# An encoder layer on one core: filling matmuls between early products, a group of w_ada loaded before the second claim, early sums and transposes moved forward, and the ramp's second half begun with the late pairs

## The chip, the cores and the metric

The kernel runs on one core of a Trainium2 chip. The metric is device time in microseconds (us). TensorE (PE in the profile) multiplies into PSUM banks, VectorE (DVE) and ScalarE (ACT) read and write SBUF and PSUM, GpSimd (POOL) and SyncE (SP) mostly issue DMAs here. Every engine works through its own queue in order; an instruction at the head of a queue that waits for a semaphore holds up all that stand behind it.

## The reference

One layer of an encoder over x (1024 tokens, 2048 channels), float32 throughout:

```python
mod = silu(c) @ w_ada + b_ada
shift, scale, gate = split(mod, 3)
h = rmsnorm(x, pre_g) * (1 + scale) + shift
q, k, v, gate_a, u, gate_p = split(h @ w_in)
y_a = windowed_gqa(q, k, v, rel_table, sink) * silu(gate_a)
y_p = multiscale_pool(u, w_pool_grp, pool_scale) * silu(gate_p)
g_a, g_p = split(sigmoid(h @ w_merge + b_merge))
o = (g_a * (y_a @ w_br_attn) + g_p * (y_p @ w_br_pool)) @ w_out
return x + gate * rmsnorm(o, post_g)
```

What the change touches is the beginning: mod, h, and the first eighth or so of `h @ w_in`.

## The kernel before, in words

**Numbers.** A float32 operand is split into a high part (rounded, by ACT) and a low part (the rest, by DVE); `split` (L95 to L97) does it. A product takes three matmuls for each 128 rows of k: high by high, high by low, low by high. All large products are Strassen products of two by two blocks (`strassen`, L223): seven block products, with sums of blocks of the weights (on DVE, as they come in) and sums of blocks of the moving operand (`B11`, `T3`, `T2`, `B21`, `T4`, `T1`, `B22`, prepared once). A pair is 256 columns of weights, and its work runs over seven steps (`run`, L336); the last block product of a pair is put off to step 2 of the next (`flush`, L331).

**The rows of k.** The 16 k tiles of h are used as pairs of tiles j = 0 to 7. The first pass over all weights uses j = 0 to 3, the second j = 4 to 7. For h of pair j the kernel needs the columns j of shift and scale, hence a product of silu(c) with group j of w_ada (`modulation`, L484, in four quarters and a column step) and, for all rows, the norms of x (`norm_rows` L414, `scale_rows` L429) and its transposes on PE (`turn_part` L436, `take_turned` L444).

**The start.** To have PE at work before all of x is loaded, the first eight pairs of weights, the ramp, are cut up:
- Pairs 0 to 3 (`AHEAD_PAIRS`) are multiplied with j = 0 alone, in plain block products of six matmuls, `plain_block` (L680), marked PB in the profile. The first token half comes first (`fill_half(0)` makes its operands, loop at L705), then the second (`fill_half(1)`, L714 to L736). Their weights come as two wide tiles (`fetch_wide`, L624; splits in `wide_weights`, L672). ACT or DVE copies each finished bank and POOL's queue stores it to `ramp_d`.
- Pairs 4 to 7 are then multiplied with j = 0 and 1 as Strassen products (loop at L747): the ramp's first half. Meanwhile groups 2 and 3 of w_ada are multiplied in (`late_sums`, L651), and `fill(2)`, `fill(3)` make the operands of j = 2 and 3.
- The ramp's second half (loop at L756) adds the rest: j = 1, 2, 3 for pairs 0 to 3 (nine matmuls a block product) and j = 2, 3 for pairs 4 to 7 (six). It reads the first half's results back from `ramp_d` (`load_parts`, L216).

After that come the other pairs of the first pass, the second pass, attention, pooling, the branches and the output product, none of them touched.

**Queues and buffers.** SP issues nearly all loads and stores, in the program's order where `keep` holds it. Two pools matter. `big` has 56 slots of 128 x 512 floats: transposed rows (12), rows of x (16 for each token half), groups 0, 1, 2 of w_ada (16 each), the operands of j (14, allotted by `claim`, L558, with a memset on POOL), the last six tiles of group 3; a slot that is asked for is that of an earlier tile, and what fills it waits for that tile's last reader. Tiles `raw` (weights as loaded) have four buffers; a pair with two k pairs takes one of them, one with three or four takes two (`load_raws`, L191). The wide tiles are two of the four.

In the order of the program SP has: x first half, wide 0, group 0, wide 1, x second half, group 1, weights of pairs 4 and 5, group 2 (behind `claim(1)`), weights of pair 6, group 3, weights of pair 7; then the stores of the first half; then the weights of all eight pairs of the second half (`ramp_raws`, L750).

Of the kernel before, what the change touches and what calls it, by code (L numbers as in the profile page):

```python
# [16 lines left out]
ALU = mybir.AluOpType  # L17
# [4 lines left out]
P = 128  # L22
# [21 lines left out]
def encoder_layer(ctx: ExitStack, tc: tile.TileContext, x, c, table, w_ada, b_ada, pre_g,  # L44
# [36 lines left out]
    def bank(tag, name="b"):  # L81
        return psum.tile([P, 512], F32, tag=tag, name=uid(name), bufs=1 if tag in SEEDED else 2)
# [8 lines left out]
    def keep(ins):  # L91

        tc.keep_in_program_order(ins)
# [334 lines left out]

    def scale_rows(si, ssq):  # L429
        keep(nc.vector.reciprocal(rstd[:, si:si + 1], ssq[:, 5:6]))  # L430
        keep(nc.vector.tensor_scalar(xts[si, 0], xts[si, 0], rstd[:, si:si + 1], None, op0=ALU.mult))
        keep(nc.scalar.activation(xts[si, 1], xts[si, 1], AF.Copy, scale=rstd[:, si:si + 1]))

    tbanks = {}

# [39 lines left out]
    def ada_slots(j, kcs=range(KT)):  # L475
        tiles = []
        for kc in kcs:
            tiles.append(slot("ada", F32, (P, 4, P)))
            load(tiles[-1].rearrange("p (g h) n -> p g (h n)", g=2),
                 w_ada[kc * P:(kc + 1) * P, 0:2 * D].rearrange("p (g n) -> p g n", g=2)  # L480
                 [:, :, j * 256:(j + 1) * 256])
        return tiles
# [136 lines left out]
    def ramp_raws(i, js):  # L619
        raws.append(load_raws(*weight_of(RAMP_ORDER[i]), rows_in_turn(0), js, True))  # L620
# [3 lines left out]
    def fetch_wide(half):  # L624

        if not wide:
            wide.extend(wp.tile([P, 4, 256], F32, tag="raw", name=uid("wide"), bufs=4) for _ in range(2))
        for kh in range(2):
            n0 = COL_K + half * 512
            keep(load(wide[kh][:, 2 * half:2 * half + 2],  # L630
                      w_in[kh * P:(kh + 1) * P, n0:n0 + 512].rearrange("p (i n) -> p i n", n=256)))

    fetch_rows_of_x(0)
    fetch_wide(0)
    ada = [ada_slots(0)]
    fetch_wide(1)
    claim(0)
    fetch_rows_of_x(1)
    ada.append(ada_slots(1))
    ramp_raws(4, (0, 1))  # L640
    ramp_raws(5, (0, 1))
    claim(1)
    ada.append(ada_slots(2))
# [28 lines left out]
    def wide_weights(i):  # L672
        hi, lo = (wp.tile([P, 2, 256], F32R, tag=t, name=uid(t), bufs=4) for t in ("whi", "wlo"))
        for kh in range(2):
            split(hi[:, kh], lo[:, kh], wide[kh][:, i], True)
        weights0[i] = hi, lo

    blocks = [0]

    def plain_block(i, nt, s, by_vector=False):  # L680

        ps = bank(("mm", "sc")[blocks[0] % 2], "PB")
        whi, wlo = (w[:, :, nt * P:(nt + 1) * P] for w in weights0[i])
        mov = (op["B11"][0], op["B21"][0]) if s == 0 else (right["B12"], op["B22"][0])
        for n, (kh, w, m) in enumerate(((0, whi, 0), (0, wlo, 0), (1, whi, 0), (1, wlo, 0), (0, whi, 1), (1, whi, 1))):
            keep(nc.tensor.matmul(ps, w[:, kh], mov[kh][m], start=n == 0, stop=n == 5, skip_group_check=True))  # L686
        blocks[0] += 1

        def put_by():
            t = ev.tile([P, 512], F32, tag="ev", name=uid("c"))  # L690
            if by_vector:
                keep(nc.vector.tensor_copy(t, ps))
            else:
                keep(nc.scalar.activation(t, ps, AF.Copy))
            nc.gpsimd.dma_start(block(ramp_d[i], 0)(f"{nt + 1}{s + 1}"), t)

        return put_by

    wide_weights(0)
    wide_weights(1)  # L700
    g0 = modulation(0, ada[0].__getitem__, True)
    for step in g0[:4]:
# [12 lines left out]
    early.close()  # L715

# [3 lines left out]
        for k in ks:  # L720
            take_turned(1, k, False)

    plain_block(0, 0, 1)()
    turn_next((2, 3))
    plain_block(0, 1, 1)()
    fill_sums(0)
    plain_block(1, 0, 1)()
    plain_block(1, 1, 1)()
    turn_next((4, 5))
    s0, s1, s2, s3, _ = modulation(1, ada[1].__getitem__, True)  # L730
    plain_block(2, 0, 1)()
    s0()
    plain_block(2, 1, 1)()
    s1()
    plain_block(3, 0, 1)()
    s2()  # L736
    last = plain_block(3, 1, 1)
    s3(last)
    turn_next((6, 7))
    for tag in SEEDED:  # L740
        hi = op["B11"][0][0]
        keep(nc.tensor.matmul(bank(tag, "OPEN"), hi[:, 0:P], hi, start=True, stop=True))
# [12 lines left out]
    pev = ramp.enter_context(pool("rampev", 6))  # L755
    for i in range(RAMP):  # L756
        run(ramp_gen((1, 2, 3) if i in A else (2, 3), i, parts[i], True), side, range(7),
            ((3, lambda i=i: parts.update({i + 1: load_parts(pev, block(ramp_d[i + 1], 0))})),)
            if i < RAMP - 1 else ())
    flush()  # L760
    ramp.close()
    ev_ctx.close()
# [224 lines left out]
    with pool("attn") as ap:  # L987
# [116 lines left out]
        def step(u, e):  # L1104
            nu = len(UNITS)
            if e == 0 and 0 <= u - LAG_V < nu:
                values(u - LAG_V)
            if e == 1 and u % 16 in (1, 3) and u < nu:
                turn_v(u % 16 // 2)
            if e == 1 and 0 <= u - LAG_T < nu:  # L1110
                turn(u - LAG_T, 0)
                turn(u - LAG_T, 1)
            if u < nu:
                if u % 16 == 0 and e == 0:
                    take_k(UNITS[u][0] * 2 // GQA)
                if u % 4 == 0:
                    split_q(e)
                scores(u, e)
            if e == 1:
                if opened:  # L1120
                    gated(*opened.pop())
                if u % 4 == 3 and u + 1 < nu:
                    fetch_q(u + 1)
                c_ = u - LAG_V + 1
                if (c_ + 1) % 16 == 0 and c_ + 1 < nu:
                    fetch_v(UNITS[c_ + 1][0] * 2 // GQA)
                if 0 <= c_ < nu:
                    if c_ % 4 == 0:
                        fetch_gate(c_)
# [530 lines left out]
```

## Time and profile before

| what | us |
|---|---|
| median of 3 runs | 2127.03 (2126.09 to 2128.45) |
| the profiled execution | 2126.26 |
| its span, first to last instruction | 2124.5 |
| DMA traffic | 474.49 MB, mean 223 GB/s |
| DMA queue of SP (q1) | 64.6% of 16 engines |

The page's first part gives each engine's busy time as a share of the span; the windows give the same for any stretch, with the granted clock of TensorE beside it; the timeline gives each group of instructions with the idle time of the engine before it and what ended that. Times in these views count from the span's start. A matmul's shown duration overlaps the next one's, so the cost of one in a row of them is the distance of their starts.

### The profile page before, as it was taken

How to read it: one execution, taken by the hardware profiler on the slowest of the kernel's cores; microseconds unless marked ns; L12 is line 12 of the kernel's file. 1: busy time of each engine (PE TensorE's matmuls, PEld its weight loads, DVE VectorE, ACT ScalarE, POOL GpSimd, SP SyncE). 2: the span in 40 equal slices, each digit the busy share in tenths (PEclk: the TensorE clock that was granted, in tenths of full speed). 3: DMA queues.
4: the chain of work that ended last, by engine and by line, in shares of the span. 5: the costliest groups of instructions: out<-in, count | busy, mean ns of one | idle time of the engine just before them, and what ended most of it. 6: DMA issues, size and time to landing. Idle time of an engine off the chain costs nothing.

```text
span 2124.5 us, 28858 instructions
## 1 busy us (share of the span) xinstructions
PE 2079.3 (98%) x9453; PEld 1706.7 (80%) x9453; DVE 1551.5 (73%) x2783; ACT 1114.9 (52%) x2118; POOL 41.7 (2%) x135
## 2 busy tenths in 40 slices
PE   6989999999999999999999999999999999999998
PEld 3568878788888888888888888888888788888886
DVE  5576768788556776677777678957957977879667
ACT  5553434444474544566666543333645645767554
POOL 1100000000000000000000000010000000000000
PEclk9899999999999999999999999999999999999999
DMA  9846877999686455545544477675754555685996
GB/s 335 302 167 213 277 252 257 316 331 299 203 262 207 133 171 203 166 165 173 176 169 156 139 232 234 220 246 178 236 169 158 186 199 192 213 320 203 296 336 242
DMA packets 304171, 474.49 MB, mean 223 GB/s; under 512 B 24323, under 2 KB 144235, under 8 KB 304020
## 3 DMA queue, kind: packets, MB, share of 16 engines
q1 hardware_dynamic: 297664, 455.70, 64.6%
q0 software_dynamic: 4896, 14.73, 1.8%
q10 hardware_dynamic: 1460, 2.22, 0.3%
q8 instruction: 74, 1.21, 0.2%
q14 instruction: 77, 0.63, 0.1%
HBM read 344.60 MB, written 130.05 MB: 223 GB/s over the span
## 4 chain that ended last, share of the span: by engine, by line
PE 92%; DVE 3%; DMA 3%; ACT 1%; issue 1%; SPq 0%; DVEq 0%; ACTq 0%
PE Z L248 30%; PE V L248 20%; PE X L248 20%; PE Z L1367 2%; PE Z L1369 2%; PE Z L1368 2%; PE V L1369 1%; PE X L1368 1%; PE X L1369 1%; PE V L1368 1%; PE V L1367 1%; PE X L1367 1%; PE GEMV L494 1%; PE PT L1077 1%; PE PB L686 1%; DMA xt<-in_x_dram 1%
## 5 line engine op out<-in xcount | busy, mean ns | idle before, releaser
L96 ACT ACTIVATE whi<-raw 128x512 fp32r<-128x512 f32 (+2 forms) x528 | 319.0, 605 | 532.0 <-PE Z L248 260.8
L97 DVE TENSOR_TENSOR wlo<-raw,whi 128x512 fp32r<-128x512 f32 (+2 forms) x528 | 344.2, 655 | 171.8 <-PE Z L248 130.2
L97 DVE TENSOR_TENSOR wlo<-wr,whi 128x512 fp32r<-128x512 f32 x224 | 150.8, 688 | 51.9 <-ACT whi L96 48.7
L96 ACT ACTIVATE whi<-wr 128x512 fp32r<-128x512 f32 x224 | 138.5, 629 | 87.6 <-DVE wlo L97 32.0
L114 DVE TENSOR_TENSOR raw<-raw,raw 128x512 f32<-128x512 f32 (+1 forms) x80 | 54.7, 683 | 82.5 <-DMA raw<-in_w_merge_dram 60.4
L248 PE MATMUL X<-B11h,whi 128*128 128x512 f32 x332 | 91.6, 394 | 8.9 <-ACT whi L96 8.2
L114 DVE TENSOR_TENSOR u<-V,u 128x512 f32<-128x512 f32 x94 | 64.6, 688 | 40.8 <-PE V L248 40.0
L248 PE MATMUL V<-T3h,whi 128*128 128x512 f32 x332 | 91.3, 394 | 1.9 <-ACT whi L96 1.6
L96 ACT ACTIVATE whi<-ws 128x512 fp32r<-128x512 f32 (+2 forms) x88 | 53.5, 608 | 72.9 <-PE X L248 65.3
L248 PE MATMUL X<-B11l,whi 128*128 128x512 f32 x332 | 91.1, 393 | 0.1
L248 PE MATMUL X<-B11h,wlo 128*128 128x512 f32 x332 | 90.7, 393 | 0.0
L248 PE MATMUL Z<-T2h,wlo 128*128 128x512 f32 x332 | 90.2, 391 | 0.5 <-DVE wlo L97 0.5
L248 PE MATMUL Z<-B22h,whi 128*128 128x512 f32 x332 | 90.6, 392 | 0.0
L248 PE MATMUL Z<-T2h,whi 128*128 128x512 f32 x332 | 90.4, 392 | 0.1
L248 PE MATMUL Z<-T1h,whi 128*128 128x512 f32 x332 | 90.5, 390 | 0.0
L248 PE MATMUL V<-T3l,whi 128*128 128x512 f32 x332 | 90.4, 391 | 0.0
L248 PE MATMUL Z<-T2l,whi 128*128 128x512 f32 x332 | 90.2, 391 | 0.0
L248 PE MATMUL X<-B21h,whi 128*128 128x512 f32 x332 | 90.2, 390 | 0.0
L248 PE MATMUL V<-T3h,wlo 128*128 128x512 f32 x332 | 90.1, 391 | 0.0
L248 PE MATMUL V<-T4l,whi 128*128 128x512 f32 x332 | 90.0, 390 | 0.1
L248 PE MATMUL V<-T4h,whi 128*128 128x512 f32 x332 | 90.1, 391 | 0.0
L248 PE MATMUL Z<-T1l,whi 128*128 128x512 f32 x332 | 89.8, 389 | 0.0
(366 smaller groups left out, 4885.7 us busy)
## 6 DMA issues: line engine op xcount, KB each, us to landing
part<-part_d SPq DMA_DIRECT2D x136, 256.0 KB, 4.6
ada<-in_w_ada_dram SPq DMA_DIRECT2D x128, 256.0 KB, 6.0
raw<-in_w_merge_dram SPq DMA_DIRECT2D x64, 512.0 KB, 5.3
wr<-ws_dS SPq DMA_DIRECT2D x60, 512.0 KB, 5.2
raw<-in_w_in_dram SPq DMA_DIRECT2D x56, 512.0 KB, 4.0
wr<-in_w_out_dram SPq DMA_DIRECT2D x48, 512.0 KB, 4.9
proj_d<-part SPq DMA_DIRECT2D x68, 256.0 KB, 2.3
sw<-in_w_out_dram SPq DMA_DIRECT2D x64, 256.0 KB, 5.1
```

What stands on the lines that cost most here:

```text
L96: ins = (nc.scalar.activation(hi, src, AF.Copy), nc.vector.tensor_tensor(lo, src, f32(hi), ALU.subtract))
L97: nc.vector.tensor_tensor(lo, src, f32(hi), ALU.subtract))
L114: return (eng or nc.vector).tensor_tensor(o, a, b, ALU.add)
L248: nc.tensor.matmul(ps, w_[:, i], op[mov][j][m_], start=fresh and i == 0 and n == 0, stop=i == nj - 1 and n == 2, skip_group_check=True)
L494: ins = nc.tensor.matmul(pv[g:g + 32, :], scz[:, kc, :], tile_of(kc), start=kc < 4, stop=kc >= 12, tile_position=(0, g))
L686: keep(nc.tensor.matmul(ps, w[:, kh], mov[kh][m], start=n == 0, stop=n == 5, skip_group_check=True))
L1077: nc.tensor.transpose(pt[:, i * P:(i + 1) * P], p[:, i * P:(i + 1) * P], ident)
L1367: nc.tensor.matmul(pb, hi, w[0], start=first, stop=False, skip_group_check=True)
L1368: nc.tensor.matmul(pb, lo, w[0], start=False, stop=False, skip_group_check=True)
L1369: nc.tensor.matmul(pb, hi, w[1], start=False, stop=last, skip_group_check=True)
```

## The change

Nothing of what is computed changes. The parts:
- **Filling matmuls.** `warm(n)` multiplies a split weight tile of pair 0 into a bank that nobody reads, n times (128 x 512 each): 3, 3 and 4 between the quarters of group 0's product, 3 behind its column step, 4 and 3 around the last transposes of the second token half. The column step of group 0 now is a step of its own (`apart`).
- **Loads.** `fetch_wide(1)` moves ahead of group 0, and group 2 of w_ada ahead of `claim(1)`.
- **Weight splits.** All four pairs' wide weights are split ahead of group 0's product; before, pairs 2 and 3 were split inside the loop over plain blocks.
- **Row scaling.** Both scaled quarters of a row of x are now scaled by DVE (before, one by DVE and one by ACT); all copies of plain blocks are now made by ACT (before, in the first token half, every second by DVE). The norm of the next rows is now issued behind a pair's plain blocks, the scaling ahead of them.
- **Plain blocks.** `plain_blocks` issues both column halves of a pair together; with `apart` (first pair of each token half) four matmuls of each column half come first and the two with a low part of the operand after.
- **Transposes and sums forward.** In the second token half the order becomes: pair 0, transposes 2 and 3, `fill_sums(0)`, pair 1, transposes 4 and 5, two quarters of group 1, pair 2, transposes 6 and 7, third quarter, the two OPEN matmuls, fourth quarter with pair 3's blocks between its product and its column step.
- **The ramp's second half** runs pairs 4, 5, 6, 7 first and then 0 to 3 (`SECOND`). Its first loads of weights are issued inside the first half, one at step 1 of pairs 5, 6 and 7 and one behind the loop; those of pairs 0 to 3 at step 1 of the third, fifth, sixth and seventh pair of the second half.

```diff
     def scale_rows(si, ssq):
         keep(nc.vector.reciprocal(rstd[:, si:si + 1], ssq[:, 5:6]))
-        keep(nc.vector.tensor_scalar(xts[si, 0], xts[si, 0], rstd[:, si:si + 1], None, op0=ALU.mult))
-        keep(nc.scalar.activation(xts[si, 1], xts[si, 1], AF.Copy, scale=rstd[:, si:si + 1]))
+        for q in range(2):
+            keep(nc.vector.tensor_scalar(xts[si, q], xts[si, q], rstd[:, si:si + 1], None, op0=ALU.mult))
...
     fetch_wide(0)
+    fetch_wide(1)
     ada = [ada_slots(0)]
-    fetch_wide(1)
...
     ramp_raws(5, (0, 1))
+    ada.append(ada_slots(2))
     claim(1)
-    ada.append(ada_slots(2))
...
-    def plain_block(i, nt, s, by_vector=False):
+    def plain_blocks(i, s, apart=False):
...
+        parts_ = ((range(4), range(4, 6)) if apart else (range(6),))
+        for ns in parts_:
+            for nt in range(2):
+                for n in ns:
+                    piece(nt, n)
+                if n == 5:
+                    put_by(nt)
+
+    def warm(n):
+
+        whi = weights0[0][0]
+        for _ in range(n):
+            keep(nc.tensor.matmul(bank("at", "WARM"), whi[:, 0, 0:P], whi.rearrange("p k n -> p (k n)"),
+                                  start=True, stop=True))
+
+    for i in range(AHEAD_PAIRS):
+        wide_weights(i)
+    g0 = modulation(0, ada[0].__getitem__, True, True)
+    for step in g0[:2]:
         step()
+        warm(3)
+    g0[2]()
+    warm(4)
+    g0[3]()
+    g0[4]()
+    warm(3)
     fill_half(0)
+    ssq = norm_rows(4)
     for m in range(4):
-        if m < 2:
-            wide_weights(2 + m)
-        ssq = norm_rows(4 + m)
-        for nt in range(2):
-            plain_block(m, nt, 0, nt == 1)()
         scale_rows(4 + m, ssq)
+        plain_blocks(m, 0, m == 0)
+        if m < 3:
+            ssq = norm_rows(5 + m)
-    for m in range(4):
-        turn_part(1, m, (0, 1), SEEDED)
+    turn_part(1, 0, (0, 1), SEEDED)
+    turn_part(1, 1, (0, 1), SEEDED)
+    turn_part(1, 2, (0, 1), SEEDED)
+    warm(4)
+    turn_part(1, 3, (0, 1), SEEDED)
+    warm(3)
     fill_half(1)
...
+    plain_blocks(0, 1, True)
     turn_next((2, 3))
     fill_sums(0)
+    plain_blocks(1, 1)
     turn_next((4, 5))
     s0, s1, s2, s3, _ = modulation(1, ada[1].__getitem__, True)
     s0()
     s1()
+    plain_blocks(2, 1)
+    turn_next((6, 7))
     s2()
-    last = plain_block(3, 1, 1)
-    s3(last)
-    turn_next((6, 7))
     for tag in SEEDED:
         hi = op["B11"][0][0]
         keep(nc.tensor.matmul(bank(tag, "OPEN"), hi[:, 0:P], hi, start=True, stop=True))
+    s3(lambda: plain_blocks(3, 1))
...
-    for i in range(AHEAD_PAIRS, RAMP):
-        run(ramp_gen((0, 1), i, None, False), side, range(7),
-            ((4, lambda: parts.update({0: load_parts(ev, block(ramp_d[0], 0))})),) if i == RAMP - 1 else ())
-    for i in range(RAMP):
+    SECOND = [*range(AHEAD_PAIRS, RAMP), *A]
+    def second_raws(n):
+        i = SECOND[n]
         ramp_raws(i, (1, 2, 3) if i in A else (2, 3))
+
+    for n, i in enumerate(range(AHEAD_PAIRS, RAMP)):
+        at = [(1, partial(second_raws, n - 1))] if n else []
+        if i == RAMP - 1:
+            at.append((4, lambda: parts.update({SECOND[0]: load_parts(ev, block(ramp_d[SECOND[0]], 0))})))
+        run(ramp_gen((0, 1), i, None, False), side, range(7), at)
+    second_raws(RAMP - AHEAD_PAIRS - 1)
     fill(2)
     fill(3)
...
+    later_raws = {2: 4, 4: 5, 5: 6, 6: 7}
+    for n, i in enumerate(SECOND):
+        at = [(3, lambda i=SECOND[n + 1]: parts.update({i: load_parts(pev, block(ramp_d[i], 0))}))] if n < RAMP - 1 else []
+        if n in later_raws:
+            at.append((1, partial(second_raws, later_raws[n])))
+        run(ramp_gen((1, 2, 3) if i in A else (2, 3), i, parts[i], True), side, range(7), at)
```

More of the change, by code (lines that the diff above doesn't have):

```diff
@@ L678, in encoder_layer, with piece, put_by @@
     blocks = [0]
-    def plain_block(i, nt, s, by_vector=False):
-        ps = bank(("mm", "sc")[blocks[0] % 2], "PB")
-        whi, wlo = (w[:, :, nt * P:(nt + 1) * P] for w in weights0[i])
+    def plain_blocks(i, s, apart=False):
+        whi, wlo = weights0[i]
         mov = (op["B11"][0], op["B21"][0]) if s == 0 else (right["B12"], op["B22"][0])
[L685 to L689, printed above, removed]
+        open_ = []
+        for nt in range(2):
+            open_.append(bank(("mm", "sc")[blocks[0] % 2], "PB"))
+            blocks[0] += 1
+        def piece(nt, n):
+            kh, w, m = ((0, whi, 0), (0, wlo, 0), (1, whi, 0), (1, wlo, 0), (0, whi, 1), (1, whi, 1))[n]
+            keep(nc.tensor.matmul(open_[nt], w[:, kh, nt * P:(nt + 1) * P], mov[kh][m], start=n == 0, stop=n == 5,
+                                  skip_group_check=True))
+        def put_by(nt):
@@ L690, in put_by @@
             t = ev.tile([P, 512], F32, tag="ev", name=uid("c"))
[L691 to L694, printed above, removed]
+            keep(nc.scalar.activation(t, open_[nt], AF.Copy))
             nc.gpsimd.dma_start(block(ramp_d[i], 0)(f"{nt + 1}{s + 1}"), t)
[L697 to L702, printed above, removed]
-        step()
+        parts_ = ((range(4), range(4, 6)) if apart else (range(6),))
@@ new lines, in plain_blocks @@
+        for ns in parts_:
+            for nt in range(2):
+                for n in ns:
[10 more added lines that the diff above has]
+    g0 = modulation(0, ada[0].__getitem__, True, True)
@@ L755, in encoder_layer @@
     pev = ramp.enter_context(pool("rampev", 6))
[L756 to L759, printed above, removed]
+    later_raws = {2: 4, 4: 5, 5: 6, 6: 7}
[4 more added lines that the diff above has]
+        run(ramp_gen((1, 2, 3) if i in A else (2, 3), i, parts[i], True), side, range(7), at)
     flush()
```

7 lines of the change are left out of this document (removed).

## The prediction

> **What bounds the kernel now.** First the page's list of engines.
>
> ```profile
> PE 2079.3 (98%) x9453; PEld 1706.7 (80%) x9453; DVE 1551.5 (73%) x2783; ACT 1114.9 (52%) x2118; POOL 41.7 (2%) x135
> ```
>
> TensorE (PE) is busy for 2079.3 of 2124.5 us. The change removes none of its products, so what can be won is in the 45 us in which it stands, and in stretches where it is busy at a lower clock. Both lie ahead of 144 us. I cut that part into windows (columns: busy time and count of PE, PEld, DVE, ACT, POOL; granted clock; DMA share and GB/s).
>
> ```profile
> 37.70:44.40 6.70, 5.70 (x13) 4.46 (x14) 4.53 (x13) 2.88 (x8) 1.12 (x2) 0.50 1.06 377
> 44.50:54.60 10.10, 8.02 (x39) 6.31 (x37) 8.07 (x25) 8.61 (x23) 3.21 (x6) 1.00 1.08 382
> 54.80:61.50 6.70, 6.12 (x18) 4.55 (x19) 4.81 (x7) 2.23 (x4) 1.01 (x12) 0.50 1.07 380
> 82.10:88.80 6.70, 6.39 (x14) 4.61 (x15) 5.50 (x10) 4.45 (x10) 0.00 (x0) 0.50 1.09 353
> 88.90:130.40 41.50, 41.50 (x217) 29.13 (x215) 31.83 (x70) 30.16 (x60) 0.00 (x0) 1.00 0.55 185
> 120.00:130.00 10.00, 10.00 (x46) 8.26 (x44) 9.59 (x19) 9.00 (x19) 0.00 (x0) 1.00 0.36 128
> 130.60:138.70 8.10, 0.01 (x1) 0.00 (x0) 1.59 (x3) 1.08 (x2) 0.00 (x0) 0.66 0.93 312
> 138.80:143.40 4.60, 4.60 (x11) 3.63 (x12) 3.33 (x7) 1.71 (x5) 0.00 (x0) 0.50 0.66 224
> ```
>
> The reader is to see four stretches of about 7 us at a granted clock of 0.50, and one of 8.1 us with no matmul at all. Half of the busy time at 0.50 is lost: 5.70/2 = 2.9, 6.12/2 = 3.1, 6.39/2 = 3.2 and 4.60/2 = 2.3 us. PE's timeline has the largest hole and what ended it (start, us, then the group, its count and the idle time before it).
>
> ```profile
> 129.54 0.61 PE L248 MATMUL Z<-T1l,whi 128*128 128x512 f32 x2
> 130.00 0.61 PE L248 MATMUL Z<-T1h,wlo 128*128 128x512 f32 x2
> 138.79 1.65 PE L248 MATMUL X<-B11h,whi 128*128 128x512 f32 x3 [8.18 <-ACT whi L96]
> 140.24 1.48 PE L248 MATMUL X<-B11l,whi 128*128 128x512 f32 x3
> ```
>
> Two matmuls start 0.46 us apart at full clock, so one costs 0.23 us; after the hole three take 1.45, twice as much each. The hole lies between the last product of the ramp's first half and the first of its second half. The chain that ended last says why ACT was late.
>
> ```profile
> 132.00 0.32 SPq L326
> ...
> 132.37 5.83 DMA raw<-in_w_in_dram
> ```
>
> The second half's first weights (`ramp_raws`, L198) are issued at 132.37, after SP has put out the last sums of the first half, and take 5.83 us. That is a load behind a queue, not a lack of compute.
>
> **The ramp's second half from the late pairs.** The changed order issues the loads of pairs 4, 5 and 6 (their k pairs 2 and 3) inside the first half, each into the buffer that the pair before has left, so the first leaves over two pairs (42 matmuls at 0.23, 9.7 us each) before its use. X of pair 4 then waits neither for SP nor for a landing. It still needs `fill(3)` and a weight split from DVE and ACT, and these are full just then (9.59 and 9.00 of 10 in 120:130). In the hole DVE does only 1.59 us of leftover. I take 0.8 us as what PE then waits, half of that. The ends are 0, and 3.8 us if the leftover and two thirds of the 3.33 us that the first, wider weights take on DVE in 138.8:143.4 come one after another. Gone with the hole is its half-rate tail: 8.18 + 2.3 - 0.8 = **9.7 us faster**, between 6.7 and 10.5. The amount of PE work does not change: late pairs have 42 matmuls and early ones 63, in either order.
>
> Behind it, three early pairs (two buffers each) get their loads one pair ahead, at step 1 of the pair before, and wait there for the buffers that are freed at step 2. A 63-matmul pair lasts 14.5 us, so some 10 us are left from issue to use. From 130 to 215 us the loads of such weights landed so (view of the tile `raw`):
>
> ```profile
> DMA to landing us min/median/max: 3.1/3.5/7.2
> ```
>
> 7.2 is under 10, so this costs nothing; if one took more, the excess would be paid up to three times.
>
> **Front: loads.** Now SP's queue ahead of the plain blocks, and the longest wait in it.
>
> ```profile
> 14.35 11.66 SPq L479 DMA_DIRECT2D ada<-in_w_ada_dram  x16
> 26.40 1.09 SPq L630 DMA_DIRECT2D wide<-in_w_in_dram  x2
> ...
> 52.41 4.73 SPq L198 DMA_DIRECT2D raw<-in_w_in_dram  x4
> 68.40 13.15 SPq L479 DMA_DIRECT2D ada<-in_w_ada_dram  x16
> ```
>
> ```profile
> SPq L479 <- PE GEMV L494: 12.5, 4, 11.0
> ```
>
> Sixteen loads of group 0 leave in 11.66 us, 0.73 each, with the DMA engines full. Putting the two `wide` loads ahead of them delays group 0's last tile by 1.5 us. PE's rows show that the modulation product is paced by those landings:
>
> ```profile
> 25.08 7.64 PE L494 MATMUL GEMV<-ada,scz 128*32 128x512 f32 x32
> 33.41 0.66 PE L462 MATMUL PM<-ident,acc 128*128 128x128 f32 x4 [0.69 <-ACT acc L501]
> 35.66 0.50 PE L686 MATMUL PB<-B11h,whi 128*128 128x512 f32 x1 [1.59 <-ACT B11h L549]
> ...
> 38.70 0.79 PE L686 MATMUL PB<-B21l,whi 128*128 128x512 f32 x1 [1.17 <-DVE B21l L117]
> ...
> 51.27 0.81 PE L441 MATMUL XT<-ident,xt 128*128 128x128 f32 x6
> 53.53 0.44 PE L441 MATMUL XT<-ident,xt 128*128 128x128 f32 x2 [1.45 <-DVE xt L431]
> 54.73 0.80 PE L686 MATMUL PB<-B12h,whi 128*128 128x512 f32 x1 [0.76 <-ACT B12h L549]
> ...
> 57.82 0.80 PE L686 MATMUL PB<-B22l,whi 128*128 128x512 f32 x1 [0.58 <-DVE B22l L117]
> ```
>
> Thirty-two matmuls took 7.64 us, where eight of group 1 take 1.06 (row below), 4.2 in all; the rest is waiting. So the first operand comes at 35.66 + 1.5: **1.5 us slower**. The third w_ada group ahead of the second claim removes the 11.0 us in which SP stood between 57 and 68 us. No wait of PE in the ramp names that group, so by itself this is worth **0**; it lets group 3 and the last first-half weights come some 10 us earlier, which keeps them off the path when the ramp starts sooner. If the claim's memsets, now later, held up `fill(1)`, that would cost; their slots come free with the third quarter of group 1, over 3 us before, so 0.
>
> **Front: filling matmuls.** There are 20, 0.23 us each, 4.6 us if nothing hid them. Ten go between the quarters of the modulation product: 4.2 + 2.3 is less than the 9.1 us it now lasts. Three go into the 1.59 us after the column transposes. Seven stand around the last transposes, where 1.45 + 0.76 us were idle. All hidden: **0**, and 4.6 the other end. What they may win is the clock.
>
> The two pieces `apart` let eight matmuls run before the first one that needs a low part, not five: three times 0.23, **0.7 us** each at 38.70 and 57.82, so 1.4 faster. Row scalings go from ACT to DVE and copies from DVE to ACT, four against four; from 44.5 to 54.6 the two are busy for 8.07 and 8.61 of 10.1, so neither is the better place: 0. The weight splits of pairs 2 and 3 leave this stretch for the idle time under the modulation product; this is in what follows.
>
> Of the two half-rate stretches here (2.9 and 3.1 us) I take one as avoided: **3.0 faster**. Ahead of the first, idle time falls from 0.7 (25.08 + 7.64 to 33.41) + 1.59 to about 1.6 us, ahead of the second from 1.45 + 0.76 to about 1.3; the clock fell after 2.2 and more, and nothing shows where the limit is, so each is a toss-up. With PE ahead, it meets the ACT and DVE chain of norms and scalings, 8 of 10 busy, sooner: I give 0.7 back. Ends: none avoided, 0; both, 5.3 net.
>
> The Trainium skill, page "TensorE: Matmul & The Clock Gate", Part 1, has the gate as a free-running window of about 3.4 us in which only a whole idle window throttles. By that rule, holes of 1.6 us would cost no clock and the fillers would be worth nothing; the granted 0.50 behind 1.59 us, with PE busy on both sides of it, speaks against it, and so I do not go by it. The sum by it would be that of rival (c).
>
> **Front: transposes and sums forward.** The tail before the ramp:
>
> ```profile
> 75.07 1.06 PE L494 MATMUL GEMV<-ada,scz 128*32 128x512 f32 x8
> ...
> 76.93 0.66 PE L462 MATMUL PM<-ident,acc 128*128 128x128 f32 x4
> 77.42 1.04 PE L441 MATMUL XT<-ident,xt 128*128 128x128 f32 x8
> 79.58 0.99 PE L742 MATMUL OPEN<-B11h 128*128 128x512 f32 x2 [1.12 <-ACT xT L449]
> 81.28 0.50 PE L248 MATMUL X<-B11h,whi 128*128 128x512 f32 x1 [0.71 <-ACT B11h L96]
> ```
>
> From the last quarter's end (76.13) to X are 5.2 us. The change takes transposes and OPEN out of this (about 1.5 us, now ahead) and ACT's copies with them, and puts twelve matmuls (2.7 us) in. But the column transposes now queue behind these twelve, so the chain of columns, modulation and split starts 2 us later. With two copies fewer on ACT in that chain the two nearly cancel: **0.4 faster**, between 1 slower and 2.5 faster. PE idles over 2 us again, so the stretch 82.1 to 88.8 stays at half rate: 0. The other end is 2.5 (3.2, less the wait for T3's operand that the slow clock now hides; 0.7 is a guess between 0 and its whole product, six matmuls or 1.4).
>
> **Sum.** +1.5 - 1.4 - 3.0 + 0.7 - 0.4 = 2.6 faster in front, 9.7 at the hole: 12.3. The profiled execution took 2126.26 us (span 2124.5 and 1.8 around it), 0.8 under the median of 2127.03; 2126.3 - 12.3 + 0.8 gives **2114.7**.
>
> **Rivals.** (a) The clock stays full in front: both stretches and that at the ramp's start go, 3.0 + 2.5 more, 17.8 in all: 2109.2. For it: 20 fillers just where the clock fell. Against: over 2 us idle still ahead of the ramp. 12%. (b) The hole closes only in part, because DVE's leftover and the first splits come in turn: 3.8 us instead of 0.8, and some 1.7 of half rate: 2119.4. For it: 9.59 of 10; against: the steady ramp ran at such loads without a hole. 12%. (c) The front wins nothing, fillers and late loads eating the rest: only 9.7, 2117.3, or with 1.5 lost 2118.8. 9%. (d) Slower: the early pairs' loads, one pair ahead, come too late three times. It decides from a landing time above 10 us; at 17 us it costs 3 x 7 = 21 and 2135.7. Longest seen: 7.2. 3%. (e) The order on the engines comes out such that the hole only moves behind pair 7: no change, 2%. My forecast has 62%.
>
> From (a) to (b): 2109.0 to 2119.5, without (d), (e) and the outer parts of (a) and (b). About 0.2% (4.3 us) is what a measurement here can tell from no change; only (d) and (e) end above 2122.8: faster 0.95, same 0.02, slower 0.03.
>
> **What would show it.** In the changed profile: X after the ramp's first half follows Z within 1 to 2 us, and no granted 0.50 there; `raw` issued inside the first half; the modulation product ends near 34.2; first PB near 37.2; ramp's X near 79; one half-rate stretch fewer. A wait of PE on `whi` at the start of an early pair would mean (d); idle time of over 2 us with DVE full, (b).

## The result and the profile after

The changed kernel takes **2112.06 us** (median of 4 runs, 2110.36 to 2113.16), the kernel before 2126.65 us beside it (4 runs, 2126.09 to 2128.45): a ratio of 0.9929, 95% interval 0.9912 to 0.9946. Forecast were 2114.7 us, between 2109.0 and 2119.5. The profiled execution took 2110.36 us with a span of 2108.6, that of before 2126.26 with 2124.5.

From the page of the changed kernel, the list of engines (busy time, share, instructions):

```profile
PE 2074.4 (98%) x9473; PEld 1704.8 (81%) x9473; DVE 1549.4 (73%) x2787; ACT 1112.1 (53%) x2114; POOL 42.2 (2%) x135
```

PE has 20 instructions more, the fillers, and is busy 4.9 us less; the windows below show less time at half clock. The timeline of PE at the place where the hole was (start, duration, group, count):

```profile
126.55 0.62 PE L248 MATMUL Z<-T1h,wlo 128*128 128x512 f32 x2
127.00 0.62 PE L248 MATMUL X<-B11h,whi 128*128 128x512 f32 x2
```

X of the second half follows the last Z of the first by 0.45 us, where before it followed by 8.79 (130.00 to 138.79). The hole is gone. The windows of the same execution (columns as in the prediction: busy time of PE, PEld, DVE, ACT, POOL, granted clock, DMA):

```profile
38.10:41.50 3.40, 3.40 (x9) 2.49 (x10) 3.16 (x7) 1.82 (x5) 0.00 (x0) 0.50 1.04 374
...
54.80:61.50 6.70, 6.17 (x33) 4.84 (x32) 5.13 (x9) 3.21 (x6) 1.07 (x2) 1.00 1.08 372
79.00:85.80 6.80, 5.81 (x14) 4.46 (x14) 5.20 (x11) 4.09 (x9) 0.00 (x0) 0.50 1.10 357
...
116.00:126.00 10.00, 10.00 (x46) 8.26 (x45) 9.96 (x22) 9.83 (x22) 0.00 (x0) 1.00 0.58 185
126.60:144.00 17.40, 17.40 (x78) 14.41 (x77) 15.78 (x35) 9.87 (x21) 0.00 (x0) 1.00 0.85 288
```

Behind the first half PE now works through 17.40 of 17.40 us at full clock, although DVE and ACT were busy for 9.96 and 9.83 of the 10 us before. Two half-rate stretches are left of the four ahead of 144 us: one of 3.4 us at 38, one of 6.8 at the ramp's start. SP's queue shows why there is no hole (start, duration, issues):

```profile
59.59 14.85 SPq L479 DMA_DIRECT2D ada<-in_w_ada_dram  x16
...
93.36 1.07 SPq L198 DMA_DIRECT2D raw<-in_w_in_dram  x2
106.19 0.94 SPq L198 DMA_DIRECT2D raw<-in_w_in_dram  x2
119.78 0.94 SPq L198 DMA_DIRECT2D raw<-in_w_in_dram  x2
...
130.36 0.93 SPq L198 DMA_DIRECT2D raw<-in_w_in_dram  x2
```

The weights that X needs at 127.00 were issued at 93.36, over 30 us ahead, and the third w_ada group leaves without the 11.0 us stand of before. The timeline of PE in front:

```profile
25.64 1.07 PE L494 MATMUL GEMV<-ada,scz 128*32 128x512 f32 x8
26.63 1.62 PE L711 MATMUL WARM<-whi 128*128 128x512 f32 x3
28.18 1.06 PE L494 MATMUL GEMV<-ada,scz 128*32 128x512 f32 x8
...
33.82 1.06 PE L494 MATMUL GEMV<-ada,scz 128*32 128x512 f32 x8
35.68 0.66 PE L462 MATMUL PM<-ident,acc 128*128 128x128 f32 x4 [0.80 <-ACT acc L501]
36.09 1.27 PE L711 MATMUL WARM<-whi 128*128 128x512 f32 x3
37.93 0.67 PE L691 MATMUL PB<-B11h,whi 128*128 128x512 f32 x1 [0.57 <-ACT B11h L549]
...
52.37 0.44 PE L441 MATMUL XT<-ident,xt 128*128 128x128 f32 x2
...
53.56 0.50 PE L691 MATMUL PB<-B12h,whi 128*128 128x512 f32 x1
...
56.66 0.50 PE L691 MATMUL PB<-B22l,whi 128*128 128x512 f32 x1 [0.53 <-DVE B22l L117]
...
76.67 0.50 PE L248 MATMUL X<-B11h,whi 128*128 128x512 f32 x1 [2.27 <-ACT B11h L96]
...
78.16 0.50 PE L248 MATMUL X<-B11l,whi 128*128 128x512 f32 x1 [0.76 <-DVE B11l L97]
...
80.12 0.77 PE L248 MATMUL V<-T3h,whi 128*128 128x512 f32 x1 [0.99 <-ACT T3h L96]
```

Where the time went: the last Z of the first half stands at 126.55 and not 130.00, so **3.45 us** were won in front of it. Z to X shrank by 8.34 us, and the half-rate tail behind it, 2.3 us by the prediction's own row, went with it: **10.6 us**. That is 14.1 of the 15.9 us between the two spans. The rest, 1.8 us, lies behind the ramp, whose instructions the change leaves alone. About half of it is one wait: at 394 us PE stood 0.87 us for DVE (`PMR<-acc`) in the execution of before, and not at all in this one. All twelve other kernels below have that wait too (0.8 to 2.2 us), so I do not count it to the change; the medians differ by 14.6.

The 3.45 us in front have two parts. Up to the first block of the second token half (B12h) the gain is only 1.17 us (54.73 to 53.56): the first blocks before it take 15.63 us in place of 19.07, 3.44 less, but they start 2.27 later (35.66 to 37.93). The other 2.28 us come behind B12h, where before had a half-rate stretch (54.8 to 61.5) and the changed kernel has none.

### The profile page after: what moved, and what is told of

It reads as the page before. It is cut to its first block, busy times and chain, and to the rows that moved or that the text cites. A ratio compares the mean times of both kernels' runs of the same rounds, so it can differ in the third digit from the quotient of the medians.

```text
span 2108.6 us, 28906 instructions
## 1 busy us (share of the span) xinstructions
PE 2074.4 (98%) x9473; PEld 1704.8 (81%) x9473; DVE 1549.4 (73%) x2787; ACT 1112.1 (53%) x2114; POOL 42.2 (2%) x135
## 4 chain that ended last, share of the span: by engine, by line
PE 95%; DVE 2%; DMA 2%; ACT 0%; issue 0%; DVEq 0%; ACTq 0%
PE Z L248 31%; PE X L248 21%; PE V L248 21%; PE Z L1394 2%; PE Z L1396 2%; PE Z L1395 2%; PE X L1395 1%; PE V L1396 1%; PE V L1395 1%; PE X L1396 1%; PE V L1394 1%; PE X L1394 1%; PE PB L691 1%; DMA xt<-in_x_dram 1%; PE PT L1104 1%; PE GEMV L494 1%
## 5 line engine op out<-in xcount | busy, mean ns | idle before, releaser
L114 DVE TENSOR_TENSOR raw<-raw,raw 128x512 f32<-128x512 f32 (+1 forms) x80 | 54.7, 683 | 86.0 <-DMA raw<-in_w_merge_dram 57.4
L248 PE MATMUL X<-B21l,whi 128*128 128x512 f32 x332 | 89.8, 390 | 0.0
L248 PE MATMUL Z<-B22l,whi 128*128 128x512 f32 x332 | 89.8, 390 | 0.0
```

The source lines that it names most:

```text
L114: return (eng or nc.vector).tensor_tensor(o, a, b, ALU.add)
L248: nc.tensor.matmul(ps, w_[:, i], op[mov][j][m_], start=fresh and i == 0 and n == 0, stop=i == nj - 1 and n == 2, skip_group_check=True)
```

## The experiments

Twelve kernels ran. Each is the changed kernel with one edit (the first two: one half of the change alone). The table has the median with its range and runs, and the ratio to the kernel before in runs on the same chip. From the profiled execution of each come three starts on PE: the first plain block (PB), the first block of the second token half (B12h), and X<-B21h, the step that follows PE's last wait for the ramp's first operands. The last column is the half-rate stretches ahead of 95 us, to a tenth.

| run | us (range, runs) | ratio, 95% | PB | B12h | X<-B21h | granted 0.50 |
|---|---|---|---|---|---|---|
| before | 2126.65 (2126.09-2128.45, 4) | | 35.66 | 54.73 | 88.87 | 37.7-44.5, 54.7-61.6, 82.0-88.9 |
| after | 2112.06 (2110.36-2113.16, 4) | 0.9929, 0.9912-0.9946 | 37.93 | 53.56 | 84.95 | 38.1-41.5, 79.1-85.9 |
| e1 front only | 2123.00 (2121.26-2125.71, 11) | 0.9981, 0.9972-0.9990 | 37.90 | 53.52 | 84.89 | 78.5-85.3 |
| e2 second half only | 2115.67 (2114.64-2117.27, 5) | 0.9949, 0.9935-0.9962 | 36.49 | 55.56 | 87.95 | 37.3-44.1, 81.6-88.5 |
| e3 loads behind the loop | 2122.23 (2119.86-2128.49, 10) | 0.9981, 0.9971-0.9990 | 38.09 | 53.72 | 84.41 | 76.8-83.6 |
| e4 no fillers | 2111.65 (2110.78-2112.82, 5) | 0.9928, 0.9915-0.9940 | 37.00 | 52.61 | 84.03 | 52.7-56.1, 76.6-83.5 |
| e5 not apart | 2112.69 (2110.28-2114.92, 5) | 0.9935, 0.9921-0.9948 | 37.42 | 53.05 | 84.98 | 78.0-84.9 |
| e6 tail as before | 2110.97 (2108.12-2114.60, 5) | 0.9925, 0.9913-0.9938 | 39.96 | 55.59 | 84.60 | 79.1-82.5 |
| e7 late fillers only | 2111.30 (2109.50-2112.34, 5) | 0.9926, 0.9913-0.9938 | 37.50 | 53.13 | 84.19 | 77.0-83.8 |
| e8 columns between blocks | 2110.34 (2109.43-2111.92, 5) | 0.9923, 0.9911-0.9935 | 38.19 | 53.81 | 82.83 | 77.3-80.7 |
| e9 third group behind claim | 2111.19 (2108.76-2112.82, 5) | 0.9929, 0.9916-0.9943 | 37.58 | 53.21 | 83.09 | 79.0-82.4 |
| e10 e8, stores by SP | 2110.36 (2110.10-2111.52, 5) | 0.9926, 0.9913-0.9938 | 37.43 | 53.06 | 82.59 | 78.2-81.7 |
| e11 e10, fillers at ramp | 2112.73 (2108.04-2115.52, 5) | 0.9930, 0.9917-0.9944 | 37.69 | 53.32 | 81.43 | 38.0-41.4 |
| e12 wide behind group 0 | 2114.21 (2110.68-2115.82, 5) | 0.9941, 0.9928-0.9953 | 39.81 | 56.77 | 88.05 | 82.3-89.1 |

### The two halves of the change, each alone

e1 keeps the changed front and takes the old second half:

```
-    SECOND = [*range(AHEAD_PAIRS, RAMP), *A]
...
+    for i in range(RAMP):
+        ramp_raws(i, (1, 2, 3) if i in A else (2, 3))
```

> The changed front, with the ramp's second half as it was before. My theory (the hole is a load that stands behind SP's stores, and front and hole add up): the hole of about 8 us with its half-rate tail comes back; of the change only the front's 3 to 4 us are left: about 2123 us, ratio 0.998. Rival (the front's earlier loads free SP sooner and so shrink the hole too): a hole under 6 us and 2120 us or less.

e2 is the kernel before with the new second half (the block from `SECOND` to `later_raws` put in its place).

> The front as before, with the changed second half of the ramp alone. My theory: no idle time of PE at the ramp's middle, 10 to 11 us faster than before: about 2116 us, ratio 0.995. Rival (closing it needs the front's earlier third group and free queue): a hole of 3 us or more stays, 2119 us or more.

Waits of PE between 60 and 260 us in e1 (who waited for whom: us in total, times, longest):

```profile
PE X L248 <- ACT whi L96: 7.7, 1, 7.7
```

and PE's timeline at the same place in e2:

```profile
129.31 0.61 PE L248 MATMUL Z<-T1h,wlo 128*128 128x512 f32 x2
129.76 0.62 PE L248 MATMUL X<-B11h,whi 128*128 128x512 f32 x2
```

Each half does what it says without the other. The front alone won 3.7 us (2126.7 to 2123.0), the second half alone 11.0 (2126.7 to 2115.67); together 14.7, and the whole change 14.6. They add up, so the front is not hidden by the hole, nor the reverse. That the sum fits to 0.1 us is closer than these spreads can tell, and e1's profiled execution lost time at a later place too: at 391.51 PE had waited 2.20 us for DVE ahead of `PMR<-acc` (0.87 in before), and 3.4 us at half rate followed, which before lacks there. How many of e1's eleven runs had this isn't known; those that did understate the front. The same place cost e3, below, 1.86 us and a half-rate stretch.

### What closes the hole: the order of pairs or the place of the loads

e3 keeps the new order, but puts all loads of the second half behind the first half's loop, so that SP reaches them after the last sums:

```
-        at = [(1, partial(second_raws, n - 1))] if n else []
+        at = []
...
-    second_raws(RAMP - AHEAD_PAIRS - 1)
+    for n in range(RAMP - AHEAD_PAIRS):
+        second_raws(n)
```

> The whole change, but the loads of pairs 4 to 7 for the second half are issued behind the first half's loop, all four together. My theory (the load's place in SP's queue made the hole): PE stands 6 to 9 us between the halves and runs at half rate after it: 2121 to 2123 us. Rival (late pairs first is what matters, since one buffer that is free early suffices): no hole over 1 us, 2112 us.

First PE's waits, then SP's timeline in e3:

```profile
PE X L248 <- ACT whi L96: 7.8, 1, 7.8
```

```profile
127.51 0.32 SPq L326 DMA_DIRECT2D ramp_d<-p  x1
127.88 8.46 SPq L198 DMA_DIRECT2D raw<-in_w_in_dram  x8
```

The hole is back at 7.8 us, with the new order of pairs in place. The loads stand behind the last `ramp_d` store in SP's queue, as they did before the change. So the place in that queue decides; the new order alone does not close the hole. That the old order could not have had early loads, because its first pair takes two of the four buffers, is argued and wasn't tried.

### The fillers

e4 issues none of the 20 (`warm` returns at once); e7 leaves out the ten between the quarters and keeps the rest.

```
-    for step in g0[:2]:
-        step()
-        warm(3)
-    g0[2]()
-    warm(4)
-    g0[3]()
+    for step in g0[:4]:
+        step()
```

> The whole change without its 20 filling matmuls. My theory (they hold the clock up): two half-rate stretches of nearly 7 us ahead of 62 us as in the kernel before, 3 to 6 us slower than the change: 2115 to 2118 us. Rival (idle time this short costs no clock, the order of the work gained the front): 2111 to 2112.5 us, the granted clock no lower than in the changed kernel.

> The whole change without the ten fillers between the quarters of group 0's product; the three behind its column step and the seven around the last transposes stay. My theory after the run without any (the ten push the last quarter back by about 0.9 us, and the idle time there does not cost the clock each time): first plain block near 37.0 instead of 37.9, 2111 to 2111.7 us. Rival (the ten are what holds the clock ahead of 45 us): half rate for 6.8 us there, 2114 us or more.

My theory fell: without them the time is 2111.65, with ten of them 2111.30, with all 2112.06, one result within the spread. PE's timeline in e4:

```profile
25.82 6.27 PE L494 MATMUL GEMV<-ada,scz 128*32 128x512 f32 x28
32.28 1.79 PE L494 MATMUL GEMV<-ada,scz 128*32 128x512 f32 x4 [0.18 <-DMA ada<-in_w_ada_dram]
34.75 0.66 PE L462 MATMUL PM<-ident,acc 128*128 128x128 f32 x4 [0.69 <-ACT acc L501]
37.00 0.50 PE L691 MATMUL PB<-B11h,whi 128*128 128x512 f32 x1 [1.59 <-ACT B11h L549]
```

The modulation product ends at 32.28 + 1.79 = 34.07 here and at 33.82 + 1.06 = 34.88 with the fillers, 0.8 us later, where they had been priced as hidden. Their share in this is open: in e7, without the ten between the quarters, the product ends at 34.57 (its last rows start at 32.01 and last 2.56, behind a wait of 0.52 for a landing), in e5, with all of them, at 34.49. In the changed kernel three of them last from 26.63 to 28.18, 0.52 each, not 0.23. The view of the tile `WARM` in the changed kernel says what they wait for:

```profile
its engine sat idle before it (us, times) until:
  PE WARM L711: 3.5, 10
```

Ten times a filler waited for the filler ahead of it, 3.5 us in all. With 4.2 us of product and 5.2 of fillers (1.55 + 1.54 + 2.10), PE and not the landings paces this stretch there.

Whether the fillers hold the clock, single executions don't settle. After 1.59 us of idle time e4 starts its blocks at full clock; after 0.80 + 0.57, with fillers between, the changed kernel dropped to 0.50. But in the table all three executions without fillers (before, e2, e4) have a half-rate stretch ahead of 62 us, and of the eleven with fillers only two (after, e11). What the times show is that a clock held there, if it was, is worth nothing that can be measured.

### What a half-rate stretch costs in the first blocks

The table shows a number that no edit moves: from PB to B12h it takes 15.61 to 15.63 us in the changed kernel and in every run that has its front, except e12. The fillers, `apart` and the clock make no difference. The same window in two executions, first the changed kernel, then e9:

```profile
37.50:45.00 7.50, 7.07 (x24) 5.53 (x25) 6.21 (x16) 5.02 (x13) 1.11 (x2) 0.77 1.04 369
```

```profile
37.50:45.00 7.50, 7.38 (x30) 5.49 (x31) 6.37 (x17) 4.83 (x14) 1.11 (x2) 1.00 1.06 371
```

At the end of these blocks e9's timeline has the wait that the changed kernel (52.37, no wait) lacks:

```profile
52.02 0.44 PE L441 MATMUL XT<-ident,xt 128*128 128x128 f32 x2 [0.97 <-DVE xt L432]
```

The full-clock execution does 30 matmuls where the other does 24, and then waits for DVE; both arrive after 15.63 us. DVE's own waits in the changed kernel, from 37.9 to 53.6 us, are for ACT alone (3.2 us), none for a landing or for PE. The last rows of the chain in its timeline, the scaling that the transposes at 52.37 need:

```profile
51.63 0.16 DVE L430 RECIPROCAL rstd<-ssq 128x1 f32<-128x1 f32 x1 [0.36 <-ACT ssq L426]
51.83 0.88 DVE L432 TENSOR_SCALAR xt<-xt,rstd 128x512 f32<-128x512 f32 x2
```

So this part is set by the norms and scalings on DVE and ACT, and 3.4 us at half clock cost nothing. Before, the same part took 19.07 us, and there DVE did wait for PE. Its timeline in before:

```profile
42.09 0.69 DVE L692 COPY c<-PB 128x512 f32<-128x512 f32 x1 [1.18 <-PE PB L686]
...
43.95 0.76 DVE L97 TENSOR_TENSOR wlo<-wide,whi 128x256 fp32r<-128x256 f32 x2 [0.57 <-ACT whi L96]
```

DVE stood 1.18 us for a plain block that it had to copy, from a PE that had itself waited 1.17 us (38.70) and ran at half clock (37.7 to 44.5), with the next scaling queued behind the copy. So in the kernel before a low clock could delay this chain, and in the changed one, where ACT makes the copies, it does not.

### The other edits of the front

e5 takes `apart` away, both times, so that each block runs its six pieces in turn.

```
-        plain_blocks(m, 0, m == 0)
+        plain_blocks(m, 0)
...
-    plain_blocks(0, 1, True)
+    plain_blocks(0, 1)
```

> The whole change with the plain blocks of both first pairs in one piece each (six matmuls, then six). My theory (three more matmuls fit into each wait for a low part): 0.7 us lost twice, about 1.4 us slower than the change: 2113.5 us. Rival (PE soon waits for the norms and scalings on ACT and DVE anyway, so nothing is lost): 2112 us within 0.5.

PE's waits between 36 and 62 us in e5:

```profile
PE PB L691 <- DVE B22l L117: 1.0, 1, 1.0
PE PB L691 <- DVE B21l L117: 0.8, 1, 0.8
```

The waits on the low parts grow from 0.5 to 1.8 us, but the one on `B21l` lies inside the 15.63 us and costs nothing; only that in the second half is paid. The time is 0.6 over the change, within the spread: a small gain of `apart` is possible, not shown.

e6 puts the tail back: the sums and the transposes behind pair 3's blocks.

```
-    s0()
-    s1()
     plain_blocks(2, 1)
-    turn_next((6, 7))
-    s2()
...
+    s0()
+    s1()
+    plain_blocks(3, 1)
+    s2()
+    s3()
+    turn_next((6, 7))
```

> The whole change with the tail ahead of the ramp in the old order (pair 2, two quarters, pair 3, two quarters with the column step, transposes 6 and 7, OPEN). My theory (matmuls moved in and transposes moved out nearly cancel): 0 to 1 us slower than the change, 2112 to 2113 us, first X of the ramp under 1 us later than the change's 76.7. Rival (the fillers being worth nothing, the front's gain was made here): 2 to 4 us slower, 2114 to 2116 us.

2110.97: the new tail is worth nothing that can be measured, as against the 0.4 us forecast. In its execution the blocks began 2.0 us later than in the changed kernel, and X<-B21h still came 0.35 earlier, with 3.4 us of half rate at the ramp in place of 6.8.

e9 puts the third w_ada group behind the second claim again, and e12 the second half of the wide loads behind group 0, with the splits of pairs 2 and 3 back in the loop.

```
-    ada.append(ada_slots(2))
     claim(1)
+    ada.append(ada_slots(2))
```

> The whole change, but the loads of the third w_ada group are issued behind the second claim again. Theory: the wait of SP behind the claim comes back (before: one stand of 11.0 us between 57 and 68) and group 3 lands about 10 us later, but no wait of PE names either, so X of the ramp stays at 76 to 78 us and the time at 2112 +- 1. Rival: the move keeps the last first-half weights off the path (as the prediction guessed in passing): then PE waits on whi in the first half, between 85 and 126 us, and the time is 2114 or more.

```
     fetch_wide(0)
+    ada = [ada_slots(0)]
     fetch_wide(1)
-    ada = [ada_slots(0)]
...
-    for i in range(AHEAD_PAIRS):
+    for i in range(2):
         wide_weights(i)
...
+        if m < 2:
+            wide_weights(2 + m)
         plain_blocks(m, 0, m == 0)
```

> The whole change, but the second half of the wide loads goes behind group 0's sixteen again, and pairs 2 and 3 are split in the loop over the first blocks, as before. Theory of the prediction: these two loads ahead of group 0 cost 1.5 us, so the modulation product ends 1.5 us earlier (at 33.4 in place of 34.9), the first PB starts at 36.4 in place of 37.9, and the time falls by up to 1.5 us, to 2110.5, less what the four splits cost on ACT and DVE in the loop. Rival: the front is held by the chain of ACT and DVE from 41 us on, so the earlier start is lost in a wait of PE on XT or B12, or the splits take it: 2112 to 2113.

e9 came out at 2111.19: the group's place is worth nothing, as forecast. e12 took 2114.21, later than both theories had it, though its interval still meets that of the change. In its timeline of PE:

```profile
27.45 1.14 PE L494 MATMUL GEMV<-ada,scz 128*32 128x512 f32 x8
...
35.70 1.06 PE L494 MATMUL GEMV<-ada,scz 128*32 128x512 f32 x8
...
39.81 0.50 PE L691 MATMUL PB<-B11h,whi 128*128 128x512 f32 x1 [0.57 <-ACT B11h L549]
...
55.58 0.44 PE L441 MATMUL XT<-ident,xt 128*128 128x128 f32 x2 [1.53 <-DVE xt L432]
...
56.77 0.50 PE L691 MATMUL PB<-B12h,whi 128*128 128x512 f32 x1
```

The product lasts 9.31 us (27.45 to 36.76), as it does in the changed kernel (9.24): paced by the fillers, it gets nothing from earlier landings. That it starts 1.8 us later is the transposes before it, whose rows came later in this execution (in e6, too, the blocks began 2 us later). From PB to B12h it is 16.96 us and not 15.63: **the splits in the loop cost 1.33 us** of the DVE and ACT chain. DVE's rows agree: twice a pair of low-part splits stands between the rows' norms, 0.67 us from start to start (45.35 to 46.02, 49.07 to 49.74), and DVE waits for no landing there, so the later loads are not the cause. That is a part of the front's gain which can be named: the splits were moved under the modulation product, where these engines are mostly idle.

### The start of the ramp

e8 runs the column step of group 1 between pair 3's two blocks. e10 adds to it that SP and not POOL issues these blocks' stores; e11 adds eight fillers ahead of X.

```
-    s3(lambda: plain_blocks(3, 1))
+    s3()
+    plain_blocks(3, 1, between=columns1)
...
-            nc.gpsimd.dma_start(block(ramp_d[i], 0)(f"{nt + 1}{s + 1}"), t)
+            (nc.sync if (i, s) == (3, 1) else nc.gpsimd).dma_start(block(ramp_d[i], 0)(f"{nt + 1}{s + 1}"), t)
...
+    for _ in range(8):
+        hi = op["B11"][0][0]
+        keep(nc.tensor.matmul(bank("at", "WARM"), hi[:, 0:P], hi, start=True, stop=True))
```

> The whole change, with the column step of group 1 issued between the two blocks of pair 3 instead of behind both. My theory (the column transposes queue behind twelve matmuls and hold up the chain to the ramp's first operand): that chain starts 1.3 us earlier, X of the ramp near 75.4, about 1.3 us faster: 2110.7 us. Rival (fill(1) on ACT and DVE, which runs behind PE there, sets the ramp's start): under 0.5 us faster.

> The column step of group 1 between pair 3's two blocks, as in the earlier run of that kind, and the two stores of these blocks issued by SP in place of POOL, so that the memsets of the second claim are not queued behind a store that waits for ACT's copy. Theory: the 0.67 us that ACT waited there for a memset of POOL goes, B11h is split at 75.8 in place of 76.42, X of the ramp starts at 76.5 in place of 77.1, and the time falls by 0.6 to about 2109.7. Rival: B11h then waits for ACT's own copy and the weight split in front of it (both lie between 74.9 and 75.8 anyway), or SP's queue holds the stores back; X stays at 77 and the time at 2110.3 +- 0.7.

> The version before it, and eight matmuls that feed nothing (0.23 us each at full clock, 1.9 in all) on PE between pair 3's last block and the ramp's X, where PE stands for over 2 us. Theory of the gate (idle time ahead of a stretch makes the half rate): the stretch at the ramp's start (3.4 to 6.8 us at 0.50, so 1.7 to 3.4 us of work lost) does not come in its profile, and the time falls by 1.5 to 3 us, to 2107 to 2108.5. Rival (as with the early fillers, whose absence cost nothing): the stretch comes as often or its loss is hidden by the wait for T3's operand, and the time is 2109.5 to 2111.

In e8 X came 6.40 us behind pair 3's first block (70.70 to 77.10), in the changed kernel 6.22 (70.45 to 76.67): the columns were ready sooner, and nothing came of it. ACT's timeline, then POOL's, in e8:

```profile
76.42 0.63 ACT L96 ACTIVATE B11h<-xT 128x512 fp32r<-128x512 f32 x1 [0.67 <-POOL T3h L563]
```

```profile
75.74 0.54 POOL L697 DMA_DIRECT2D ramp_d<-c  x1 [1.91 <-ACT c L696]
76.27 0.12 POOL L563 MEMSET B11h<- 128x1 f32 x1
```

The claim's memsets stood behind a store that waited for ACT's copy, and the split of the first operand waited for the memsets. In e10 they ran at once, and X came 5.63 us behind the block (69.95 to 75.58), 0.77 us sooner, where 0.6 to 0.7 had been expected. POOL's timeline, then PE's:

```profile
67.95 0.12 POOL L563 MEMSET B11h<- 128x1 f32 x1
```

```profile
75.58 0.50 PE L248 MATMUL X<-B11h,whi 128*128 128x512 f32 x1 [1.67 <-ACT B11h L96]
...
78.54 0.76 PE L248 MATMUL V<-T3h,whi 128*128 128x512 f32 x1 [1.00 <-ACT T3h L96]
```

The time did not follow (2110.36 after 2110.34). V still came 0.56 us sooner behind the block (8.59, in e8 9.15), though it now waited 1.00 us for its operand (in e8 0.31); but X<-B21h came 12.64 us behind it and not 12.13, as e10's half-rate stretch starts later and slows V and Z, where that of e8 slows X too. So the gain went partly into the next operand's wait and partly into the place of a half-rate stretch. e11's profile is the only one with no half rate at the ramp:

```profile
74.00:90.00 16.00, 14.94 (x67) 10.10 (x70) 13.42 (x27) 11.81 (x25) 0.00 (x0) 1.00 1.10 349
```

Its X<-B21h is the earliest of all, 81.43, but its five runs spread from 2108.04 to 2115.52 with a median of 2112.73, at a mean granted clock of 0.998 or 0.999 in all five, so the clock does not explain the spread. Theory and rival both stay possible there; a gain of such fillers isn't shown. No version beat the change by more than its spread.

## Why the prediction was right

- **The hole: 9.7 us forecast, 10.6 in the profile, 11.0 by e2.** The mechanism was right: loads behind SP's stores, shown by e3. The term mis-sized is the 0.8 us that PE was to wait for DVE's leftover and the first splits. It was 0, the other end given: at 9.96 of 10 busy, DVE still had the split ready when Z ended.
- **Loads one pair ahead for the early pairs: 0 forecast, 0 found.** PE's waits from 84 to 260 us in the changed kernel are an empty list.
- **Wide loads ahead of group 0: 1.5 us slower.** The size is bracketed only: without fillers the product's end moved from 32.72 (before, 25.08 + 7.64) or 33.56 (e2, whose front is that of before, 27.24 + 6.32) to 34.07 (e4). With fillers it was 34.88 and the first PB 37.93, not 34.2 and 37.2. That the fillers cost 0 was not so between the quarters, where they wait for one another, 0.52 us each; what they add to the end is up to 0.8 (e4), and by e7 perhaps nothing.
- **One half-rate stretch avoided by fillers, 3.0 us faster: this reason was wrong, and that the front came out near is luck.** Without any fillers (e4), or with ten of them (e7), the time is the same within its spread. Up to B12h the front won 1.17 us: 3.44 in the first blocks, less the later start of 2.27. Two steps failed here. The chain of norms and scalings, priced at 0.7 us given back, sets the end of the first blocks (after and e9: 15.63 us both), so in the changed kernel a half-rate stretch and a stall in there cost nothing. And the weight splits that left this chain got no term in the sum; they are worth 1.33 us (e12). For the other 2.1 us DVE's timeline of before has candidates: the waits of 1.18 us for a block to copy and of 0.57 for ACT's split are both gone. The scalings on DVE are none: in the changed kernel the rows' norms start 3.05 us apart, in before the last ones 2.79 and 2.99. No run takes these apart.
- **What came behind B12h: 2.28 us.** The second stretch (54.7 to 61.5) is gone after the change, but it is also missing in e2, whose front is that of before, and from B12h to X<-B21h e2 is 1.75 us shorter than before (32.39 and 34.14): so much of the 3.45 us in the two profiles need not be the change's. Nor has such a stretch a fixed price: e4 has one of 3.4 us at 52.7 and takes 31.42 us there, the changed kernel 31.39.
- **`apart`: 1.4 forecast.** One of the two stalls lies in that chain and was worth 0; the time moved by 0.6 (e5), within the spread.
- **Tail: 0.4 forecast, nothing measurable (e6).** X came at 76.67, not 79, but B11l and T3h then kept PE for 0.76 and 0.99 us: the operands come one by one, so an earlier X isn't an earlier ramp. That the half-rate stretch stays at the ramp's start was right.
- **Third w_ada group: 0, right (e9).** The claim's memsets did not hold up `fill(1)` in the changed kernel; e8 shows that they do as soon as the columns come sooner, since they stand behind stores in POOL's queue.

In sum, the front was forecast at 2.6 us and gave 3.7 (e1), the hole at 9.7 and gave 11.0. Rival (a), the clock full in front, fell: it is not full, and in the first blocks a low one costs nothing. Rivals (b), (d) and (e) had their waits named, and none is in the profile; (c), no gain in front, is excluded by e1, whose interval ends at 0.9990.

## What to carry to other kernels

When a queue first puts out the results of one phase and then fetches the next phase's inputs, reorder the next phase so that it starts with work whose buffers are already free, and issue those loads inside the phase before. Ahead of a matmul engine with gaps, look for the chain on the other engines that ends the stretch: in the one found here a lower clock, a filler and a shorter stall were all worth nothing, and work taken off that chain counted. Price a filler by its own spacing in a trace, not by that of a pipelined product.

## What was not expected of the hardware

The granted clock differs between executions of much the same work. Ahead of 38 us the changed kernel and e9 have the same rows on PE (0.80 us idle ahead of PM, 0.57 ahead of PB); one then ran 3.4 us at 0.50, the other none. All half-rate stretches ahead of 150 us last 3.4, 6.8 or 10.2 us (10.2 at the hole, in before and in e1), whole multiples of about 3.41. The Trainium skill, page "TensorE: Matmul & The Clock Gate", Part 1, has a free-running window of 3413 ns, which these lengths bear out, and a return to half rate after a whole idle window, with which these traces differ: the longest idle time ahead of the stretch at 79 us was 2.27 us. By that rule fillers in such gaps are worth nothing; by the times of e4 and e7 they were.

The same filler cost twice as much in one place as in another: 0.52 us each between the quarters, against 0.27 for e11's eight (2.14 us from 73.54 to 75.68, by its timeline of PE). In the kernel the fillers' bank has two buffers, and the modulation product holds one of them while its fillers run; that each filler therefore waits for the one ahead is argued from this, not shown.
